# A decoder trunk on one core: sums of weight blocks in the MLPs moved from VectorE into accumulating DMAs

## The chip, the cores and the metric

The kernel runs on one core of one Trainium2 chip. The metric is the device time of one execution, in microseconds, and the median over the runs is given. The kernel is one program with fp32 inputs and outputs; TensorE (PE) works on fp32r operands, each value split into a high and a low part.

## The reference, cut to what matters

Two layers, the first with latent attention (MLA), the second with gated linear attention (GLA), each followed by an MLP on a residual stream of 512 tokens by 1024 channels:

```python
def sq_relu_mlp(xn, w_up, w_down):          # (512,1024), (1024,4096), (4096,1024)
    hid = jnp.square(jax.nn.relu(xn @ w_up))
    return hid @ w_down

for i in range(DEPTH):                       # DEPTH = 2
    ...
    x = x + mix.astype(x.dtype)
    x = x + sq_relu_mlp(rms_norm(x, norm_mlp[i]), mlp_w_up[i], mlp_w_down[i]).astype(x.dtype)
return rms_norm(x, final_norm)
```

Only the two MLPs are touched by the change.

## The kernel before, in words

**Split products.** An fp32 operand is split by `split`: ScalarE (ACT) copies it to a high part in fp32r (line 112), VectorE (DVE) subtracts that from the operand to get the low part (line 115). A product is then three matmuls: high by high, high by low, low by high. `piece` does this for a weight slice, into buffers `wh` and `wl` of which there are three each.

**Seven products in place of eight.** In each MLP both matrix products are done by a Winograd form of Strassen's scheme on 2 x 2 blocks: the tokens are cut into a first and a second half, the 1024 channels into two halves, and a weight block of `FB` = 512 hidden columns into two halves of 256. The weight blocks are called a11, a12, a21, a22. Seven products of blocks and of sums of blocks give the four results. The sums of the token side (T1 to T4, made by `combine` and `combined`) are formed once for each MLP, with the norm's gains in them; the sums of the weight side are formed for each block, on VectorE:

- step s5: s = a21 + a22 (line 904)
- step s6: s = s - a11 (line 919)
- step s3: a12 = a12 - s (line 925)
- step s7: a21 = a11 - a21 (line 932)

`up_block(b)` gives the steps of hidden block b (0 to 7): s1 (product with a11), s5, s2 (with a12), s6, s3, s7, s4 (with a22). A product of an up step is 24 matmuls of 256 columns (line 818). Steps s6, s7 and s4 add to one PSUM bank (`b2`), and VectorE reads it in between: after s7 (line 935) for one result, after s4 for the other. `finish` applies the norm's factor, the max with zero (line 862, VectorE) and the square (line 863, ScalarE).

`down_block(s)` does the same for the second product, with the hidden blocks 2s and 2s+1, in seven steps of 48 matmuls each: p1, p5, p6, p7, p2, p3, p4. Its weight quarters are 512 x 512 and are called "11", "21", "12", "22"; the sums over them are in p5 (line 987: S = 21 + 22), p6 (line 992), p7 (line 1004: 21 = 11 - 21) and p3 (line 1019). `operand` splits the hidden side into one of two buffers, h1 and h0 in turn. Only blocks 0 to 5 go this way; blocks 6 and 7 are multiplied plainly by `down` and `down_final`.

**Order.** In `mlp`, blocks 0 and 1 come first: s0 (their a11 and a12 are split early), then s1 of both, the last channel tile's token sums, the norm's mean and its factor, then s2 of both; then the rest of block 0, of block 1, and so on. From block 2 on a down step is put in behind every second up step, and one behind s4 of odd blocks. In blocks 0 and 1 there is none. The order of the instructions on each engine is fixed when the program is built; VectorE and ScalarE work through theirs in order, and the DMA queues of SyncE (SP) and GpSimd (POOL) too.

**Loads.** All weights come by SP's queue. Up slices (a11, a12, a21, a22, 512 KB each) go into five buffers `raw` of the pool `up`, one of which is also taken for s in each block. For blocks 0 and 1, a21 and a22 come together as one transfer of 1 MB each (line 1116) into two of the three `raw` buffers of the pool `down_w`; the third takes the first down quarter (line 950), and further quarters (1 MB each) take the three in turn. POOL's queue carries two small loads at the start of the program (`pos_i`, `invf`).

**Places.** `PADS` are unused bytes that shift the pools behind them. In the program before, h1 and h0 both start at 192 mod 512 bytes of their partition, the weight slices `wh` and `wl` at 416, the token operands of the up products (x, T) at 96, the `raw` buffers of `down_w` at 416.

Of the kernel before, what the change touches and what calls it, by code (L numbers as in the profile page):

```python
# [49 lines left out]
def trunk_kernel(ctx: ExitStack, tc: tile.TileContext, t_in: dict, out: bass.AP, out_row: bass.AP):  # L50
# [39 lines left out]

    PADS = dict(stage=224, right=64, up=320, masks=256, keep=128, hidden=(0, 0), down_w=(224, 224))

# [7 lines left out]
    opened_stage()  # L100
    pad(opened("edge", "right"), PADS["right"])
    opened("wide", "right")
# [163 lines left out]
    class QuadNorm(Norm):  # L266
# [36 lines left out]
        def difference(self, k):  # L303
            DVE.tensor_tensor(xT[k][:, second], xT[k][:, second], xT[k + KH][:, second], ALU.subtract)

# [480 lines left out]
    def out_proj(w2d, X, nxt, after, begun=None):  # L786
        for c in range(4):
            if c == 0:
                ps_, rest = begun or out_start(w2d, X, 0)
                rest()  # L790
            else:
                w = out_cols(w2d, c)
                if c == 3:
                    next(after)
                ps_ = [bank("ac"[c % 2]), bank("ac"[c % 2])]
                for j in range(2):
                    a_type(ps_[j], w[j], X)
            for j in range(2):
                m = c + j * KH
                DVE.tensor_tensor(xT[m], ps_[j], xT[m], ALU.add)  # L800
                nxt.add(m, xT[m])
            if c < 3:
                nxt.pair(c)
                nxt.difference(c)


    def mlp(layer, nrm, nxt, final=False):
# [5 lines left out]
        def wide_raw():  # L813
            return pool_of("down_w").tile([P, 4, 512], F32, tag="raw", bufs=3, name=uname("raw"))

        def matmuls(p, w, k0, ks, ms, x, begin, end):
# [18 lines left out]

        Q, wide, turn = {}, {}, [0, 1]

        def up_block(b):
# [7 lines left out]
            def unit(half, trail):  # L846
                if half and b < 2:
                    return wide[b][:, trail * KH : trail * KH + KH]
                t = up.tile([P, KH, 256], F32, tag="raw", bufs=5, name=uname("raw"))
                c0 = b * FB + half * 256  # L850
                with tc.issue_after(wide["last"].ins) if wide else nullcontext():
                    SP.dma_start(t, w_up[trail * 512 : trail * 512 + 512, c0 : c0 + 256].rearrange("(k p) n -> p k n", p=P))
                return t

            def product(p, a, name, begin):
# [3 lines left out]
            def finish(c, half, tk):  # L859
                qs = q[tk is second][:, 2 * half : 2 * half + 2]  # L860
                r = nrm.rstd[:, tk].unsqueeze(1).to_broadcast([P, 2, TH])
                DVE.scalar_tensor_tensor(qs, c, 0.0, r, ALU.max, ALU.mult)  # L862
                ACT.activation(qs, qs, AF.Square)  # L863
# [36 lines left out]
            def s5():  # L900
                s = v["s"] = up.tile([P, KH, 256], F32, tag="raw", bufs=5, name=uname("raw"))
                if "a12" not in v:
                    v["a12"] = unit(0, 1)
                DVE.tensor_tensor(s, v["a21"], v["a22"], ALU.add)  # L904
# [11 lines left out]
            def s6():  # L916
                if b == 1:
                    seed(v["p1"])
                DVE.tensor_tensor(v["s"], v["s"], v["a11"], ALU.subtract)
                product(v["b2"], v["s"], "T2", False)  # L920
# [3 lines left out]
            def s3():  # L924
                DVE.tensor_tensor(v["a12"], v["a12"], v["s"], ALU.subtract)  # L925
                product(v["x5"], v["a12"], "22", False)
# [4 lines left out]
            def s7():  # L931
                DVE.tensor_tensor(v["a21"], v["a11"], v["a21"], ALU.subtract)  # L932
                product(v["b2"], v["a21"], "T3", False)
# [10 lines left out]
        def down_block(s):  # L944
            last = s == NB // 2 - 2

            def quarter(dh, fh):
                t = wide_raw()
                r0 = (2 * s + fh) * FB
                SP.dma_start(t, w_dn[r0 : r0 + FB, dh * 512 : dh * 512 + 512].rearrange("(k p) n -> p k n", p=P))  # L950
                return t
# [9 lines left out]
            def product(n, a, t, evac=None):  # L961
# [11 lines left out]
                elif begin and n in (2, 3, 4, 5):  # L973
                    DVE.tensor_tensor(acc[n], p4, acc[n], ALU.add)
                else:
# [9 lines left out]
            def p5():  # L985
                v["21"], v["S"] = quarter(1, 0), quarter(1, 1)
                DVE.tensor_tensor(v["S"], v["21"], v["S"], ALU.add)
                DVE.tensor_tensor(b11, b12, b11, ALU.subtract)  # L988
                product(5, v["S"], b11)

            def p6():
                DVE.tensor_tensor(v["S"], v["S"], v["11"], ALU.subtract)
                DVE.tensor_tensor(b11, b22, b11, ALU.subtract)

# [8 lines left out]
            def p7():  # L1003
                DVE.tensor_tensor(v["21"], v["11"], v["21"], ALU.subtract)
                DVE.tensor_tensor(b12, b22, b12, ALU.subtract)
# [12 lines left out]
            def p3():  # L1018
                DVE.tensor_tensor(v["S"], v["12"], v["S"], ALU.subtract)
                product(3, v["S"], b22)  # L1020

            def p4():
                a = quarter(1, 1)
                DVE.tensor_tensor(b21, b21, b11, ALU.subtract)
                product(4, a, b21)
# [16 lines left out]
        def down(b, hid):  # L1042
            for c in range(2):
                raw = raw_rows(b, c)
                for g in range(2):
# [3 lines left out]
                    for j in range(2):  # L1049
                        m = c * 4 + g * 2 + j  # L1050
                        p = bank("b")
                        a_type(p, w, hid, cols=slice(j * P, (j + 1) * P))
                        DVE.tensor_tensor(xT[m], p, xT[m], ALU.add)
                        if b == NB - 1:
# [58 lines left out]
        for b in range(2):  # L1113
            t = wide[b] = wide_raw().rearrange("p a (b n) -> p (a b) n", b=2)
            c0 = b * FB + 256
            wide["last"] = SP.dma_start(t, w_up[:, c0 : c0 + 256].rearrange("(k p) n -> p k n", p=P))
        kept = tc.keep_in_program_order
# [8 lines left out]
        nrm.finish()  # L1126
        nrm.difference(KH - 1)
        for b in range(2):
# [421 lines left out]
    turns = rope_turns()  # L1550

    O, begun = mla(0, nrm, w0, mla_pools)
# [161 lines left out]
```

## Time and profile before

| | |
|---|---|
| median of 3 runs | 1080.58 us (1080.05 to 1083.18) |
| the profiled execution's own time | 1080.79 us |
| its span, first to last instruction | 1079.1 us |
| instructions of VectorE | 1210, busy 890.0 us |
| bytes read from HBM | 104.64 MB |
| stretch of the first MLP, of the second | about 190 to 470 us, about 743 to 1025 us |

The profile is one execution. A busy share of an engine is an average over stages of different kinds; the windows (busy time of each engine in a stretch) are the view by stage. An idle time stands with what ended it. Matmuls are pipelined: a row's duration of about 0.28 us is longer than the distance to the next one's start.

### The profile page before, as it was taken

What the parts mean: (1) busy time and instruction counts of PE and PEld (TensorE: products, weight loads), DVE (VectorE), ACT (ScalarE), POOL (GpSimd) and SP (SyncE); (2) the same over time, 40 slices, a digit from 0 to 9 for tenths busy, and PEclk for the clock granted to TensorE, in tenths of its full rate; (3) what the DMA queues carried; (4) which work ended last, traced back from release to release, by engine and by line L of the source; (5) the groups of instructions that cost most, each with busy time, mean ns of one, the idle gap of its engine ahead of it and who ended that gap; (6) DMA issues with size and microseconds to landing.
All of it is one profiled execution on the core that took longest, in us unless ns stands there. A gap on an engine that the chain in (4) does not pass through costs nothing.

```text
span 1079.1 us, 17824 instructions
## 1 busy us (share of the span) xinstructions
PE 1058.9 (98%) x7322; PEld 977.1 (91%) x7322; DVE 890.0 (82%) x1210; ACT 640.2 (59%) x934; POOL 44.5 (4%) x78
## 2 busy tenths in 40 slices
PE   9999999989999999999999999999899999999997
PEld 7788888989999999988788888888899999999986
DVE  6789879999899899967565655678999899899865
ACT  6577655566667776644334735655565667766734
POOL 6400000000000000030000000000000000000000
PEclk9999999999999999999999999999999999999999
DMA  7312017143433433260222222234324423522412
GB/s 211 95 49 79 13 31 229 42 136 99 157 98 99 157 100 96 86 203 24 62 67 78 79 79 57 61 98 138 117 79 129 146 82 134 176 76 82 137 39 79
DMA packets 97969, 107.88 MB, mean 100 GB/s; under 512 B 8048, under 2 KB 72832, under 8 KB 97888
## 3 DMA queue, kind: packets, MB, share of 16 engines
q1 hardware_dynamic: 95872, 105.52, 31.1%
q8 instruction: 57, 0.93, 0.4%
q10 hardware_dynamic: 1952, 1.21, 0.4%
q0 software_dynamic: 64, 0.02, 0.1%
q14 instruction: 24, 0.20, 0.1%
HBM read 104.64 MB, written 2.10 MB: 99 GB/s over the span
## 4 chain that ended last, share of the span: by engine, by line
PE 84%; DVE 11%; issue 2%; ACT 2%; DMA 1%; SPq 0%; DVEq 0%; ACTq 0%
PE ps L818 39%; PE ps L120 12%; PE ps L122 12%; PE ps L121 12%; DVE wl L115 4%; PE ps L137 2%; PE ps L1371 2%; DMA wraw_ckv<-in_mla_w_in_dram 1%; DVE q L862 1%; DVE h L115 1%; DVE raw L925 1%; ACT wh L112 1%; DVE raw L932 1%; DVE raw L904 0%; PE ps L1408 0%
## 5 line engine op out<-in xcount | busy, mean ns | idle before, releaser
L112 ACT ACTIVATE wh<-raw 128x1024 fp32r<-128x1024 f32 x208 | 218.9, 1057 | 155.2 <-PE ps L818 84.3
L115 DVE TENSOR_TENSOR wl<-raw,wh 128x1024 fp32r<-128x1024 f32 x208 | 251.8, 1218 | 16.6 <-ACT wh L112 16.3
L818 PE MATMUL ps<-h,wh 128*128 128x256 f32 x1344 | 170.6, 279 | 0.0
L818 PEld LDWEIGHTS ps<-h,wh 128*128 128x128 f32 x1344 | 163.0, 188 | 0.0
L818 PE MATMUL ps<-h,wl 128*128 128x256 f32 x672 | 92.3, 279 | 2.1 <-DVE wl L115 2.1
L120 PE MATMUL ps<-set,wh 128*128 128x512 f32 x232 | 92.0, 397 | 0.7 <-ACT set L245 0.7
L121 PE MATMUL ps<-set,wh 128*128 128x512 f32 x232 | 91.2, 393 | 0.6 <-DVE set L246 0.6
L122 PE MATMUL ps<-set,wl 128*128 128x512 f32 x232 | 91.1, 393 | 0.0
L112 ACT ACTIVATE wh<-wraw 128x1024 fp32r<-128x1024 f32 x41 | 43.0, 1056 | 74.0 <-PE ps L122 41.5
L818 PEld LDWEIGHTS ps<-h,wl 128*128 128x128 f32 x672 | 84.5, 188 | 2.5 <-DVE wl L115 2.5
L863 ACT ACTIVATE q<-q 128x512 f32<-128x512 f32 x64 | 40.0, 629 | 46.4 <-DVE q L862 46.2
L120 PE MATMUL ps<-wh,set 128*128 128x512 f32 x144 | 59.7, 414 | 0.0
L115 DVE TENSOR_TENSOR wl<-wraw,wh 128x1024 fp32r<-128x1024 f32 x41 | 50.3, 1230 | 10.7 <-ACT wh L112 10.6
L115 DVE TENSOR_TENSOR h<-q,h 128x1024 fp32r<-128x1024 f32 x44 | 53.6, 1220 | 4.9 <-ACT h L112 4.9
L122 PE MATMUL ps<-wh,set 128*128 128x512 f32 x144 | 56.3, 391 | 0.0
L121 PE MATMUL ps<-wl,set 128*128 128x512 f32 x144 | 56.3, 391 | 0.0
L121 PEld LDWEIGHTS ps<-set,wh 128*128 128x128 f32 x232 | 44.0, 190 | 10.5 <-DVE set L246 1.3
L120 PEld LDWEIGHTS ps<-set,wh 128*128 128x128 f32 x232 | 43.9, 190 | 10.0 <-ACT set L245 1.0
L122 PEld LDWEIGHTS ps<-set,wl 128*128 128x128 f32 x232 | 44.0, 190 | 9.0
L112 ACT ACTIVATE h<-q 128x1024 fp32r<-128x1024 f32 x44 | 46.2, 1052 | 4.8 <-DVE q L988 2.1
L818 PE MATMUL ps<-T0h,wh 128*128 128x256 f32 x128 | 33.2, 283 | 7.1 <-DVE q L935 6.7
L120 PE MATMUL ps<-hh,wh 128*128 128x512 f32 x96 | 37.4, 389 | 0.0
(512 smaller groups left out, 2778.2 us busy)
## 6 DMA issues: line engine op xcount, KB each, us to landing
raw<-in_mlp_w_down_dram SPq DMA_DIRECT2D x38, 1024.0 KB, 5.2
raw<-in_mlp_w_up_dram SPq DMA_DIRECT2D x56, 512.0 KB, 3.9
wraw<-in_gla_w_in_dram SPq DMA_DIRECT2D x11, 1024.0 KB, 5.1
wraw<-in_mla_w_o_dram SPq DMA_DIRECT2D x8, 512.0 KB, 4.8
raw<-in_mlp_w_up_dram SPq DMA_DIRECT2D x4, 1024.0 KB, 8.0
wraw<-in_gla_w_o_dram SPq DMA_DIRECT2D x8, 512.0 KB, 4.9
xT<-in_x_dram SPq DMA_DIRECT2D x6, 256.0 KB, 7.5
wraw_qn<-in_mla_w_uq_dram SPq DMA_DIRECT2D x6, 256.0 KB, 3.4
```

Source lines behind the costliest of these rows:

```text
L112: raised.append(order(ACT.activation(hi, src, AF.Copy)))
L115: return lo_eng.tensor_tensor(lo, src, f(hi), ALU.subtract)
L120: PE.matmul(psum, wh, xh, start=start, stop=False, **kw)
L121: PE.matmul(psum, wh, xl, start=False, stop=False, **kw)
L122: PE.matmul(psum, wl, xh, start=False, stop=stop, **kw)
L137: PE.transpose(psum, src, ident[: src.shape[0], : src.shape[0]])
L818: return PE.matmul(p[:, m * TH : (m + 1) * TH], w[i][:, k - k0, m * P : (m + 1) * P], x[k][j], start=start, stop=stop, skip_group_check=True,)
L862: DVE.scalar_tensor_tensor(qs, c, 0.0, r, ALU.max, ALU.mult)
L863: ACT.activation(qs, qs, AF.Square)
L925: DVE.tensor_tensor(v["a12"], v["a12"], v["s"], ALU.subtract)
L932: DVE.tensor_tensor(v["a21"], v["a11"], v["a21"], ALU.subtract)
L1371: PE.matmul(p[:, t * 64 : (t + 1) * 64].rearrange("p (n c) -> p n c", c=m), k[:, sl], later, start=True, stop=True)
```

## The change

The weight sums of s5 (blocks 0 and 1), of s7 (all blocks) and of p7 are no longer made by VectorE. Instead the second summand is read from HBM once more by a DMA on POOL's queue that adds it to what stands in the buffer (`accum_op=ALU.add`). The DMA adds, so a21 becomes a11 + a21 where it was a11 - a21, and signs are turned round elsewhere: on the token side (`combine` takes the negated gains `less`, `difference` becomes `total`), in `finish` (min with zero for half of the columns, since the square follows), in the sums of p4, p5, p6, p3, and where results are added to x. Two of these become a `scalar_tensor_tensor` with -1.0 in place of a `tensor_tensor`.

For blocks 2 to 7 the DMA goes out behind s5's sum, which reads a21. For blocks 0 and 1 all is loaded ahead, in `fill_sums`: s gets a21 by SP and then a22 added by POOL; a second buffer gets a21 and then a11 added; a third gets a22. These six halves fill all three `raw` buffers of `down_w`. The gains negated (`less`) are made once, early in the program, by one VectorE instruction of 16 columns. Pads: `right` goes, its 64 bytes being those of `less`; `hidden` becomes 416 bytes in the first MLP and 160 in the second, put between h1 and h0; `down_w` becomes 0 and 64.

```diff
-    PADS = dict(stage=224, right=64, up=320, masks=256, keep=128, hidden=(0, 0), down_w=(224, 224))
+    PADS = dict(stage=224, up=320, masks=256, keep=128, hidden=(416, 160), down_w=(0, 64))
...
+            l1, l2 = (less[:, self.g0 + j : self.g0 + j + 1] for j in (k, k + KH))
...
-            DVE.scalar_tensor_tensor(t2, u[:, first], g1, t3, ALU.mult, ALU.add)
-            DVE.scalar_tensor_tensor(t4, v[:, first], g2, t2, ALU.mult, ALU.subtract)
-            DVE.scalar_tensor_tensor(t1, v[:, second], g2, t2, ALU.mult, ALU.subtract)
+            DVE.scalar_tensor_tensor(t2, u[:, first], l1, t3, ALU.mult, ALU.subtract)
+            DVE.scalar_tensor_tensor(t4, v[:, first], l2, t2, ALU.mult, ALU.subtract)
+            DVE.scalar_tensor_tensor(t1, v[:, second], l2, t2, ALU.mult, ALU.subtract)
...
+            def fill(t, half, trail):
+                with tc.issue_after(wide["last"].ins) if "last" in wide and b > 1 else nullcontext():
+                    i = SP.dma_start(t, rows(half, trail))
+                if half and b < 2:
+                    wide["last"] = i
+                return t
+
+            def fill_sums(s):
+                v["s"] = s
+                fill(s, 1, 0)
+                joint(s, 1, 1)
+                fill(wide[b][0], 1, 0)
+                joint(wide[b][0], 0, 0)
+                fill(wide[b][1], 1, 1)
+
+            def joint(t, half, trail):
+                POOL.dma_start(t, rows(half, trail), accum_op=ALU.add)
...
             def s5():
-                s = v["s"] = up.tile([P, KH, 256], F32, tag="raw", bufs=5, name=uname("raw"))
-                if "a12" not in v:
+                if "s" not in v:
+                    v["s"] = up.tile([P, KH, 256], F32, tag="raw", bufs=5, name=uname("raw"))
                     v["a12"] = unit(0, 1)
-                DVE.tensor_tensor(s, v["a21"], v["a22"], ALU.add)
+                    DVE.tensor_tensor(v["s"], v["a21"], v["a22"], ALU.add)
+                    joint(v["a21"], 0, 0)
+                s = v["s"]
...
             def s7():
-                DVE.tensor_tensor(v["a21"], v["a11"], v["a21"], ALU.subtract)
                 product(v["b2"], v["a21"], "T3", False)
...
             def p5():
                 v["21"], v["S"] = quarter(1, 0), quarter(1, 1)
                 DVE.tensor_tensor(v["S"], v["21"], v["S"], ALU.add)
-                DVE.tensor_tensor(b11, b12, b11, ALU.subtract)
+                POOL.dma_start(v["21"], rows(0, 0), accum_op=ALU.add)
+                DVE.tensor_tensor(b11, b11, b12, ALU.subtract)
...
             def p7():
-                DVE.tensor_tensor(v["21"], v["11"], v["21"], ALU.subtract)
...
         for b in range(2):
-            t = wide[b] = wide_raw().rearrange("p a (b n) -> p (a b) n", b=2)
-            c0 = b * FB + 256
-            wide["last"] = SP.dma_start(t, w_up[:, c0 : c0 + 256].rearrange("(k p) n -> p k n", p=P))
+            wide[b] = halves(wide_raw())
+        for b, t in enumerate(halves(wide_raw())):
+            fills[b](t)
```

More of the change, by code (lines that the diff above doesn't have):

```diff
@@ L100, in trunk_kernel @@
     opened_stage()
-    pad(opened("edge", "right"), PADS["right"])
+    less = opened("edge", "right").tile([P, 16], F32, name="gains_less")
     opened("wide", "right")
@@ L834, in matmuls @@
                 one(1, 0, k, m, False, end and k == 3)
[L836 removed]
+        Q, wide, turn, fills = {}, {}, [0, 1], []
         def up_block(b):
@@ L918, in s6 @@
                     seed(v["p1"])
-                DVE.tensor_tensor(v["s"], v["s"], v["a11"], ALU.subtract)
+                DVE.tensor_tensor(v["s"], v["s"], v["a11"], ALU.add)
                 product(v["b2"], v["s"], "T2", False)
@@ L924, in s3 @@
             def s3():
-                DVE.tensor_tensor(v["a12"], v["a12"], v["s"], ALU.subtract)
+                DVE.tensor_tensor(v["a12"], v["a12"], v["s"], ALU.add)
                 product(v["x5"], v["a12"], "22", False)
@@ L973, in product @@
                 elif begin and n in (2, 3, 4, 5):
-                    DVE.tensor_tensor(acc[n], p4, acc[n], ALU.add)
+                    DVE.tensor_tensor(acc[n], p4, acc[n], ALU.add if n < 4 else ALU.subtract)
                 else:
@@ L1018, in p3 @@
             def p3():
-                DVE.tensor_tensor(v["S"], v["12"], v["S"], ALU.subtract)
+                DVE.tensor_tensor(v["S"], v["12"], v["S"], ALU.add)
                 product(3, v["S"], b22)
@@ L1052, in down @@
                         a_type(p, w, hid, cols=slice(j * P, (j + 1) * P))
-                        DVE.tensor_tensor(xT[m], p, xT[m], ALU.add)
+                        DVE.tensor_tensor(xT[m], p, xT[m], ALU.subtract if b < NB - 1 and m >= KH else ALU.add)
                         if b == NB - 1:
@@ L1550, in trunk_kernel @@
     turns = rope_turns()
+    DVE.tensor_scalar(less, gains[:, GAIN_COL["mlp"] : GAIN_COL["mlp"] + 16], -1.0, None, ALU.mult)
     O, begun = mla(0, nrm, w0, mla_pools)
```

35 lines of the change are left out of this document (21 added, 14 removed).

## The prediction

> **What bounds the kernel now.** I read the page's busy times and chain first, then a table of windows over the two MLPs, then TensorE's waits.
>
> ```profile
> PE 1058.9 (98%) x7322; PEld 977.1 (91%) x7322; DVE 890.0 (82%) x1210; ACT 640.2 (59%) x934; POOL 44.5 (4%) x78
> PE 84%; DVE 11%; issue 2%; ACT 2%; DMA 1%; SPq 0%; DVEq 0%; ACTq 0%
> ```
>
> TensorE (PE) is busy 98% of the span, so whatever the change takes from VectorE (DVE) counts only where PE stands still for it. The chain gives VectorE 11%. The windows show where (columns: length, then PE, weight loads, VectorE, ScalarE, POOL busy with counts, granted clock, DMA share, GB/s):
>
> ```profile
> 203.00:217.00 14.00, 11.77 (x99) 11.38 (x98) 14.00 (x16) 7.60 (x10) 0.00 (x0) 1.00 0.33 93
> 217.00:233.00 16.00, 14.45 (x122) 14.11 (x123) 15.93 (x17) 11.31 (x14) 0.00 (x0) 1.00 0.57 184
> 233.00:300.00 67.00, 67.00 (x585) 67.00 (x584) 62.47 (x57) 39.87 (x46) 0.00 (x0) 1.00 0.35 111
> 431.00:446.00 15.00, 13.93 (x121) 13.73 (x120) 15.00 (x15) 9.23 (x13) 0.00 (x0) 1.00 0.23 72
> 750.00:770.00 20.00, 17.54 (x145) 16.78 (x143) 19.95 (x22) 10.76 (x15) 0.00 (x0) 1.00 0.22 58
> 770.40:774.50 4.10, 4.10 (x22) 4.10 (x23) 3.85 (x4) 2.51 (x3) 0.00 (x0) 0.60 0.95 319
> 788.00:872.00 84.00, 84.00 (x732) 84.00 (x732) 78.22 (x72) 50.34 (x58) 0.00 (x0) 1.00 0.36 114
> 872.00:909.00 37.00, 36.74 (x315) 36.46 (x315) 36.90 (x33) 26.08 (x30) 0.00 (x0) 1.00 0.27 86
> 987.00:1001.00 14.00, 13.33 (x116) 13.13 (x114) 14.00 (x14) 8.23 (x11) 0.00 (x0) 1.00 0.23 76
> ```
>
> At the front of each MLP (203 to 233, 750 to 788) and at its end (431 to 446, 987 to 1001) VectorE is full and PE has holes; between them (233 to 300, 788 to 872) PE is full and VectorE has 5 to 6 us in hand. There a matmul of 256 columns starts every 67.00 / 585 = 114.5 ns, and nothing that VectorE saves shortens that. One row is odd: in 770.4 to 774.5 the granted clock is 0.60, right behind a hole of PE. TensorE's own waits, and the chain where it runs on VectorE:
>
> ```profile
> PE ps L818 <- DVE q L935: 6.7, 4, 2.0
> PE ps L818 <- DVE wl L115: 2.4, 3, 1.1
> PE ps L818 <- ACT wh L112: 1.4, 3, 0.5
> ```
> ```profile
> 200.03 1.13 DVE raw L932
> ...
> 232.66 198.91 PE ps L818 x1726
> ...
> 439.52 1.13 DVE raw L932
> ...
> 444.65 1.14 DVE wl L115
> ...
> 881.03 2.20 DVE raw L1004
> ```
>
> These ten waits (10.5 us) are what the MLPs can give back, beside the slow clock. L932, an instruction that the change drops, stands in the chain at the front and at the end; one such costs 1.13 us of chain.
>
> **The change part by part.** Removed from VectorE:
>
> ```profile
> L932 DVE TENSOR_TENSOR raw<-raw,raw 128x1024 f32<-128x1024 f32 x16 | 19.5, 1219 | 0.1
> L904 DVE TENSOR_TENSOR raw<-raw x4: 1217/1218/1222, 198.2 to 761.5; 128x1024 f32<-128x1024 f32 x4
> L1004 DVE TENSOR_TENSOR raw<-raw,raw 128x2048 f32<-128x2048 f32 x6 | 13.7, 2283 | 0.0
> ```
>
> 16 sums of step s7, 4 sums of s5 (blocks 0 and 1 of each MLP) and 6 of the down step p7: 19.5 + 4.9 + 13.7 = 38.1 us of VectorE, 19 per MLP. Most of it lies where PE is full, and is worth nothing. Wait by wait:
>
> ```profile
> 217.02 0.36 PE L818 MATMUL ps<-T0h,wh 128*128 128x256 f32 x1 [1.77 <-DVE q L935]
> L935 DVE TENSOR_TENSOR q<-ps,mt x16: 679/683/686, 216.2 to 1011.8; 128x512 f32<-128x512 f32 x16
> 445.84 0.62 PE L818 MATMUL ps<-h,wl 128*128 128x256 f32 x3 [1.07 <-DVE wl L115]
> ```
>
> (1) L935, four times, 6.7 us: s4 of blocks 0 and 1 may not add to its bank before VectorE has read it (L935), and in these blocks no down step lies between s7 and s4. Even with VectorE free, PE must wait for the 0.68 of L935 and some 0.2 of hand-over: 0.9 each, 3.6 stay and 3.1 go. In front of them four instructions go per MLP (two L904, two L932), 4 x 1.13 = 4.5 us of a VectorE that is late by 0.7 to 1.1, so I take it as in time.
> (2) L115, three times, 2.4 us: two are the ends at 445 and 1001 (1.07 each), behind the L932 of block 7; 1.13 less covers them. The third (before 909) has an L932 and L1004 ahead of it. An idle row understates a wait, since a matmul's row lasts 0.28 and the next could start 0.114 after it: 0.165 more each, so 2.4 + 0.5, less 0.3 left over: 2.6.
> (3) L112, three times: 1.4 + 0.5 = 1.9, ScalarE waiting behind L904 and L925, which come 1.1 to 4.5 us earlier. All goes.
> (4) The slow clock: 4.10 x 0.40 = 1.6 us lost, behind the longest hole (2.0). With holes of 0.9 I expect none; bounds 0 and 1.6.
> Together 9.2 us, at most 12.1 with the waits of (1) gone too, at least 4.5 if only (2) and (3) go.
>
> Added: 26 accumulating transfers on POOL's queue, 20 of 512 KB and 6 of 1 MB, and plain ones on SP's: for blocks 0 and 1 six of 512 KB in place of two of 1 MB. No row shows an accumulating transfer. The nearest:
>
> ```profile
> raw<-in_mlp_w_down_dram SPq DMA_DIRECT2D x38, 1024.0 KB, 5.2
> raw<-in_mlp_w_up_dram SPq DMA_DIRECT2D x56, 512.0 KB, 3.9
> raw<-in_mlp_w_up_dram SPq DMA_DIRECT2D x4, 1024.0 KB, 8.0
> pos_i<-in_positions_dram POOLq DMA_DIRECT2D x1, 2.0 KB, 4.5
> invf<-in_inv_freq_dram POOLq DMA_DIRECT2D x1, 16.0 KB, 6.9
> ```
>
> Ends for 512 KB: 3.9 (plain) and 3.9 + 6.9 = 10.8 (plain behind POOL's slowest issue). I take 3.9 + 4.5 = 8.4. The Trainium skill's "DMA: Bandwidth & Descriptors" (Anatomy of one DMA — SWDGE (gpsimd) path) fits 2.0 us plus bytes / 436 GB/s, an estimate of 3.2 us for a plain 512 KB; no run here shows one from this queue, and it would change nothing below.
>
> What hides them: from block 2 on the sum of s5 is read by s7 at least two up products (2.7 us each) and two down products (5.6 each) later, some 16 us, and for the down step likewise; 8.4 (or about 10 for 1 MB) fits. POOL's queue holds nothing else in the MLPs. In the first blocks the chain is longer:
>
> ```profile
> 177.35 1.00 SPq L1116 DMA_DIRECT2D raw<-in_mlp_w_up_dram  x2
> 214.56 0.37 SPq L950 DMA_DIRECT2D raw<-in_mlp_w_down_dram  x1
> ```
> ```profile
> 203.08 0.28 PE L818 MATMUL ps<-T0h,wh 128*128 128x256 f32 x1
> ```
>
> The first fill goes out at 177.35 and lands at the latest 8.0 later, 185.4. Then POOL's four accumulates follow: in series at 8.4 they land at 193.8, 202.2, 210.6 and 219.0. PE's 24-matmul products take 24 x 0.1145 = 2.75 us; the one that reads block 0's s starts at 203.08 and block 1's, five products on, at 216.8. Splitting takes 2.5 us ahead of a product, so the deadlines are 201 (s), 208 (its s7), 214 and 222: all met, with 3 us at the least. Both third-buffer halves are now taken by s, so the first down quarter waits for a buffer until 214.6, which is when the second was issued before; its product begins at 241. Cost taken: 0. The 18 MB of second reads fit a DMA share of 0.35. `less` is one small VectorE instruction early on, shorter than the 0.68 of a 512-wide one (I take 0.1). The sign changes keep each instruction's kind and count.
>
> The buffers' places: in the program before, both h buffers lie at 192 mod 512 and the weight slices at 416 (288 apart), the up operands at 96 (192 apart). The pads 416 and 160 move the second h buffer to 192 apart in MLP one and 448 in MLP two; the title's 288 is then the first buffer, unmoved. The first row is two h pieces, the second two up products, 48 matmuls each:
>
> ```profile
> 240.94:246.55 5.61, 5.61 (x51) 5.61 (x50) 5.61 (x6) 2.70 (x4) 0.00 (x0) 1.00 0.01 3
> 246.55:252.00 5.45, 5.45 (x50) 5.45 (x49) 5.45 (x5) 3.81 (x6) 0.00 (x0) 1.00 0.31 98
> ```
>
> 116.9 against 113.5 ns. In MLP one 10 of 21 operands, 480 matmuls, go to the faster distance: 480 x 3.4 = 1.6 us less. For 448 there is no row: between 1.6 less and 1.6 more, taken as 0. By the Trainium skill's "TensorE: Matmul & The Clock Gate" (Step-by-step: what each phase is for) loading the next weights takes no read bandwidth from the running matmul; by that the pads are worth 0 and the sum is 1.6 us slower. The two rows differ by 3.4 ns with PE full in both, so I go by the rows.
>
> Sum against the profiled execution's 1080.79 (span 1079.1, so 1.7 around it): 9.2 + 1.6 - 0.1 = 10.7 less, 1070.1. The median of the runs is 0.2 lower: 1069.9.
>
> **The rivals.**
> R1, only part of the stalls goes. VectorE's order is fixed when the kernel is built, and another order around L935 may keep those four waits and the slow clock: 4.5 + 1.6 goes, 1074.7. For it: L935 is bound to PE's own end. Against: VectorE loses 4.5 us of work before it.
> R2, more goes: the places are worth more (448 as good as 192) and all of (1) vanishes: 12.1 + 3.2, 1065.5.
> R3, nothing moves: what VectorE gives, another wait takes, or the second buffer in MLP two is as far off as the first gained; within 3 us of 1080.6.
> R4, slower: the accumulates come late. In series they are in time as long as each takes under some 9 us; past that the fourth is late by 4 t - 36.6 in each MLP. Both MLPs' lateness eats the 10.7 at t = 10.5, and at 12 us each it is 2 x 11.4 = 23 against 10.7: 1092. The same place has a harsher form: POOL cannot put out transfers while VectorE is busy, and in 203 to 217 it is busy 14.00 of 14.00. Then block 1's s, due at 214, comes at 233 or so, 19 late twice: 1108. "SBUF — State Buffer" of the Trainium skill (SBUF: two separate sides) has this trap for VectorE's 2-port modes, and says elsewhere that tensor_tensor has none. An L904 takes 1218 ns for 1024 elements, no doubled rate, which is against the harsh form; the long end of the bound, 10.8, is for the mild one.
>
> **How the numbers follow.** Forecast as reckoned (1066 to 1073.5): 0.53. R1 (1073.5 to 1077.3): 0.16. R2 (under 1066): 0.11. R3: 0.08. R4: 0.12. A measurement of this kernel can tell some 0.3%, 3.2 us, from no change, so faster 0.53 + 0.16 + 0.11 = 0.80, same 0.08, slower 0.12. The range leaves out R4, most of R3 and the far end of R2: 1063 to 1078.
>
> **What would show it.** L932 and L1004 as sums gone from VectorE's groups, its busy time near 852; POOL's queue with 16.8 MB more. Right: the front windows with PE full but for four holes near 0.9 us, the ends without the 1.07, no stretch of clock 0.60. The second h buffer's pieces in MLP one at 113.5 ns, and in MLP two a new number between 110 and 120. Wrong: PE or ScalarE waiting for a DMA of raw between 200 and 230, the accumulates' landings over 9 us; or the four L935 waits still near 1.7.

## The result, and the profile after

The changed kernel takes 1072.65 us (median; 1071.37 to 1073.91), against 1080.89 for the kernel before on the same chip: a ratio of 0.992 (95% interval 0.990 to 0.9941), 8.2 us faster. The forecast was 1069.9. The profiled execution has a span of 1070.3 us, 8.8 less than before.

The page of the changed kernel: busy times, the accumulating queue, and the four groups of transfers of the MLPs' weights (count, size, median us from issue to landing).

```profile
PE 1052.6 (98%) x7322; PEld 971.6 (91%) x7322; DVE 856.6 (80%) x1185; ACT 640.3 (60%) x934; POOL 77.7 (7%) x104
...
q0 software_dynamic: 13792, 16.80, 10.2%
...
raw<-in_mlp_w_down_dram SPq DMA_DIRECT2D x38, 1024.0 KB, 5.1
raw<-in_mlp_w_up_dram SPq DMA_DIRECT2D x68, 512.0 KB, 5.3
...
raw<-in_mlp_w_up_dram POOLq DMA_DIRECT2D x20, 512.0 KB, 6.5
raw<-in_mlp_w_down_dram POOLq DMA_DIRECT2D x6, 1024.0 KB, 9.2
```

VectorE lost 33.4 us of busy time, and TensorE only 6.3. (The lengths of VectorE's rows add up to 38.1 us less, as reckoned; neighbouring rows overlap at their ends, which busy time counts once and the expected 852 left out.) The transfers that now do the sums land in 6.5 and 9.2 us. TensorE's waits inside the MLPs (us in total, times, longest); L963 is the old L935, L937 the copy of the T1 product:

```profile
PE ps L825 <- DVE q L963: 4.8, 4, 1.5
...
PE ps L825 <- ACT mt L937: 0.9, 1, 0.9
...
PE ps L825 <- DVE wl L115: 0.7, 2, 0.3
```

The two large waits at the MLPs' ends are down to 0.3 each and ScalarE's L112 is gone from the list. But the four waits for L963 still take 4.8 of their 6.7 us, and one for L937 is new.

Where the 8.8 us went is read by setting TensorE's matmuls side by side: both programs issue the same 7322 in nearly the same order, so the start of the k-th in one less its start in the other is the gain up to there. The forecast's terms stand beside it:

| stretch | measured, us less | forecast |
|---|---|---|
| front of MLP one (198 to 237 us) | 0.6 | 2.2 |
| front of MLP two (744 to 797) | 3.3 | 4.4 |
| full stretches, MLP one / MLP two | 1.5 / 1.4 | 1.6 / 0 |
| ends of both MLPs, and 889 to 913 | 2.9 | 2.6 |
| before MLP one and behind MLP two | 0.8 more | 0.1 more |

(The fronts' 3.1 of L935 is halved here, of the 1.9 of L112 one wait in three is MLP one's, and the 1.6 of the slow clock is MLP two's: 6.6 in all, against 3.9.) A hole below is the distance between two matmuls' starts less one matmul's own, so it is some 0.165 us longer than the same wait in a list of waits. The last row is scatter for the most part: the first 73 us alone differ by up to 2 us between profiles of kernels that are identical there. Numbers for a stretch below leave it out.

The full stretches, where nothing waits, in windows of TensorE alone (length, busy time with matmuls started, clock, DMA share, GB/s). Before:

```profile
300.00:430.00 130.00, 130.00 (x1131) 1.00 0.36 114
810.00:890.00 80.00, 80.00 (x697) 1.00 0.38 120
```

After:

```profile
300.00:430.00 130.00, 130.00 (x1140) 1.00 0.55 146
810.00:890.00 80.00, 80.00 (x702) 1.00 0.53 146
```

The same 130 us hold nine matmuls more, 114.0 ns each and not 114.9, at the same full clock. That is the buffers' places; the second reads of the weights (DMA share 0.36 to 0.55) cost nothing there. From the starts of the 24 matmuls of each product: operands in the second hidden buffer went from 116.8 to 113.3 ns in MLP one (distance 192) and 113.8 in MLP two (448); the first buffer, unmoved at 288, stayed at 116.75. The 113.8 is a mean of two values: 18 of the 20 products take 113.3, and the last two, behind the hole at the MLP's end, 117.8.

### The profile page after: what moved, and what is told of

It reads as the page before. It is cut to its first block, busy times and chain, and to the rows that moved or that the text cites. A ratio compares the mean times of both kernels' runs of the same rounds, so it can differ in the third digit from the quotient of the medians.

```text
span 1070.3 us, 17930 instructions
## 1 busy us (share of the span) xinstructions
PE 1052.6 (98%) x7322; PEld 971.6 (91%) x7322; DVE 856.6 (80%) x1185; ACT 640.3 (60%) x934; POOL 77.7 (7%) x104
## 5 line engine op out<-in xcount | busy, mean ns | idle before, releaser
L112 ACT ACTIVATE wh<-raw 128x1024 fp32r<-128x1024 f32 x208 | 219.6, 1058 | 145.5 <-PE ps L825 98.0
L115 DVE TENSOR_TENSOR wl<-raw,wh 128x1024 fp32r<-128x1024 f32 x208 | 251.3, 1219 | 25.7 <-ACT wh L112 25.3
L112 ACT ACTIVATE wh<-wraw 128x1024 fp32r<-128x1024 f32 x41 | 43.0, 1056 | 78.0 <-PE ps L122 41.5
L878 POOL DMA_DIRECT2D raw<-in_mlp_w_up_dram x20 | 25.8, 1290 | 706.0 <-DVE raw L931 342.6
L115 DVE TENSOR_TENSOR h<-q,h 128x1024 fp32r<-128x1024 f32 x44 | 53.7, 1221 | 9.4 <-ACT h L112 9.4
L115 DVE TENSOR_TENSOR wl<-wraw,wh 128x1024 fp32r<-128x1024 f32 x41 | 50.4, 1231 | 10.6 <-ACT wh L112 10.5
L121 PEld LDWEIGHTS ps<-set,wh 128*128 128x128 f32 x232 | 43.6, 188 | 10.7 <-DVE set L246 1.7
L112 ACT ACTIVATE h<-q 128x1024 fp32r<-128x1024 f32 x44 | 46.1, 1049 | 0.6 <-DVE q L1020 0.6
```

Source lines behind the costliest of these rows:

```text
L112: raised.append(order(ACT.activation(hi, src, AF.Copy)))
L115: return lo_eng.tensor_tensor(lo, src, f(hi), ALU.subtract)
L121: PE.matmul(psum, wh, xl, start=False, stop=False, **kw)
L878: POOL.dma_start(t, rows(half, trail), accum_op=ALU.add)
```

## The experiments

All times are medians; ratios are to the kernel before in the same session, with their 95% intervals. The changed kernel's is 0.992 (0.990 to 0.9941). The sessions ran on different chips (the kernel before took 1080.9 to 1081.6 us in those with more than one execution), so small differences are read from the traces. The planner is the program that fixes each engine's order when the kernel is built.

**The places undone.**

```
-    PADS = dict(... hidden=(416, 160), down_w=(0, 64))
+    PADS = dict(... hidden=(0, 0), down_w=(224, 224))
```

> The changed kernel with the two places as before (hidden pads 0 and 0, down_w 224 and 224); all DMA accumulates stay. Theory A, the places are worth 1.6 us in MLP one and 1.4 us in MLP two, because the second hidden buffer's matmuls fell from 116.8 to 113.3 and 113.8 ns: about 1075.6 us, 3.0 above the changed kernel, growing evenly along the full stretches, with that buffer back at 116.8 ns. Rival B, the places are worth nothing and the 3 us are a side effect of the accumulates (fewer VectorE reads): 1072.6, and the second buffer stays near 113.5 ns. The prediction's own taking (1.6 and 0): 1074.2.

1074.04 us, ratio 0.9931 (0.9919 to 0.9943). Its full stretches:

```profile
300.00:430.00 130.00, 130.00 (x1131) 1.00 0.54 145
810.00:890.00 80.00, 80.00 (x698) 1.00 0.53 146
```

The count is back at 1131 with the DMA share still 0.54, and both buffers are at 116.75 ns. The running difference grows by 1.7 us in MLP one and 1.6 in MLP two: theory A, 3.2 us in all. The time alone, 1074.04, would have spoken for the prediction's own taking (1074.2). It shows about half, because the new wait at L937 is gone in this kernel (1.2 us): nothing but the addresses was changed, yet the order that the planner gives VectorE at the front came out otherwise.

**The first two blocks' sums back on VectorE.**

```
-                    joint(v["a21"], 0, 0)
+                    if b > 1:
+                        joint(v["a21"], 0, 0)
...
             def s7():
+                if b < 2:
+                    DVE.tensor_tensor(v["a21"], v["a11"], v["a21"], ALU.add)
...
-            wide[b] = halves(wide_raw())
-        for b, t in enumerate(halves(wide_raw())):
-            fills[b](t)
+            t = wide_raw()
+            wide[b] = halves(t)
...
+            wide["last"] = SP.dma_start(joined(t), w_up[...])
```

> The changed kernel, but the sums of the first two blocks of each MLP are made on VectorE again, from two 1 MB loads as before; the later accumulates and the places stay. Theory A, read from the distance between the two kernels' matmuls: the fronts brought 0.4 us in MLP one and 3.1 in MLP two (the slow clock at 770 to 774 us among them): about 1076.1 us. Rival B, the prediction's split: both fronts brought 6.6 us together (3.1 + 1.9 + 1.6), so about 1079. Rival C, MLP one's front brought more than 0.4 and lost it to the late rsqrt: 1077, with 1.08 us of wait at 209 us gone and larger waits before it.

1075.02 us, ratio 0.9935 (0.9922 to 0.9948); the span is 3.3 longer, 0.8 of it in MLP one's front and 2.4 in MLP two's. Theory A, a little short; the prediction's 6.6 for the fronts is too much. Its waits, and a window with the clock (the last three columns are clock, DMA share, GB/s):

```profile
PE ps L825 <- DVE q L967: 5.9, 4, 1.8
...
PE ps L825 <- DVE wl L115: 1.4, 2, 1.1
PE ps L825 <- ACT wh L112: 0.9, 2, 0.5
```
```profile
214.00:218.00 4.00, 2.15 (x18) 1.95 (x17) 4.00 (x6) 1.69 (x2) 0.00 (x0) 1.00 0.65 224
218.00:222.00 4.00, 4.00 (x23) 4.00 (x22) 2.44 (x4) 1.84 (x3) 0.00 (x0) 0.57 0.56 176
```

ScalarE's L112 waits are back, and so is a stretch at a low clock (0.57 over the 4 us), this time in MLP one, again behind a hole of 2.0 us. MLP one's 0.8 is a difference: the wait at L937 is gone (1.2 gained by 211 us), as rival C expected, and 2.0 is lost between 211 and 237 us, most of it to the low clock. Taking four sums per MLP off the front was worth only 1.1 us of the four L963 waits (5.9 against 4.8).

**The sums of blocks 2 to 5 and of the first two down blocks back on VectorE**, then the up sums alone.

```
-                    joint(v["a21"], 0, 0)
+                    if b > 5:
+                        joint(v["a21"], 0, 0)
...
             def s7():
+                if 1 < b < 6:
+                    DVE.tensor_tensor(v["a21"], v["a11"], v["a21"], ALU.add)
...
-                POOL.dma_start(v["21"], rows(0, 0), accum_op=ALU.add)
+                if last:
+                    POOL.dma_start(v["21"], rows(0, 0), accum_op=ALU.add)
...
             def p7():
+                if not last:
+                    DVE.tensor_tensor(v["21"], v["11"], v["21"], ALU.add)
```

> The changed kernel, but the sums of blocks 2 to 5 and those of the first two down blocks are made on VectorE again (8 up sums of 1.13 us and 4 down sums of 2.2 us over both MLPs, some 18 us of VectorE's time). Theory A, PE is full there and VectorE has slack: 1072.6 us, no change beyond 0.5. Rival B, every sum that VectorE sheds counts somewhere because its queue is what PE waits for: up to 18 us, 1090. Rival C, the accumulates cost something in the full stretch (longer landing times of the loads behind them): faster than the changed kernel, about 1071.

1077.11 us, ratio 0.9959 (0.9944 to 0.9973), span 5.1 longer: not nothing, and far from 18. The last stretch before the end of MLP two (PE, weight loads, VectorE, ScalarE, POOL), this kernel first, then the changed one:

```profile
870.00:910.00 40.00, 38.90 (x336) 38.53 (x335) 39.90 (x36) 27.99 (x34) 0.00 (x0) 1.00 0.27 81
```
```profile
870.00:910.00 40.00, 40.00 (x352) 40.00 (x352) 38.27 (x35) 28.46 (x33) 1.28 (x1) 1.00 0.56 156
```

Here VectorE had slack only until about 870 us: with the sums it is busy 39.90 of 40, as in the kernel before, and TensorE stands 1.1 us; by the running difference the stretch costs 1.9 (idle time understates a hole, and the three products between its holes run at 117.8 ns and not at 113.3). The rest is 0.3 us at 354, 1.7 in both fronts (2.3 at the last wait for the old L935, 0.6 of it got back, for the most part because MLP two's front leaves 117.8 ns at 768 us and not at 781), and 1.2 ahead of MLP one's first product, where VectorE's order came out otherwise.

> The changed kernel with the up sums of blocks 2 to 5 on VectorE again (8 of 1.13 us over both MLPs); the four down sums stay with the DMA. With both kinds back the span was 5.1 us longer: 1.2 before MLP one's first sum, 2.3 at the T3 sums of block 1, 2.0 between 354 and 906 us. Theory A, VectorE's queue is full between 870 and 910 us when it does both (39.90 of 40 us), and the down sums of 2.3 us are what fills it: the 2.0 us go, about 1075. Rival B, the planner's order moves with any sum put back, whatever the load: some other set of 0.5 to 1.2 us waits, 1072 to 1077, with VectorE not full where they lie. Rival C, the up sums count as they did: 1077.5 with the same waits.

1076.1 us, ratio 0.9939 (0.9926 to 0.9952); the profiled execution is the slowest of the six (1072.87 to 1077.63). The losses at 354 and in 870 to 910 are gone (theory A for those; VectorE is busy 39.86 of 40 there and TensorE full), those at the fronts' last wait stayed (theory C for those). VectorE at that place, start and length of each row, with block 2's sum on it:

```profile
229.91 1.23 DVE L963 TENSOR_TENSOR raw<-raw,raw 128x1024 f32<-128x1024 f32 x1
231.04 0.69 DVE L958 TENSOR_TENSOR q<-ps,mt 128x512 f32<-128x512 f32 x1
231.64 1.22 DVE L115 TENSOR_TENSOR wl<-raw,wh 128x1024 fp32r<-128x1024 f32 x1
232.78 0.69 DVE L889 SCALAR_TENSOR_TENSOR q<-q,rstd 128x512 f32<-128x512 f32 x1
233.38 1.23 DVE L115 TENSOR_TENSOR h<-q,h 128x1024 fp32r<-128x1024 f32 x1
234.51 0.69 DVE L966 TENSOR_TENSOR q<-ps,mt 128x512 f32<-128x512 f32 x1
```

and in the changed kernel:

```profile
228.21 1.22 DVE L115 TENSOR_TENSOR h<-q,h 128x1024 fp32r<-128x1024 f32 x1
229.35 0.68 DVE L957 TENSOR_TENSOR q<-ps,mt 128x512 f32<-128x512 f32 x1
229.95 1.22 DVE L115 TENSOR_TENSOR wl<-raw,wh 128x1024 fp32r<-128x1024 f32 x1
231.08 0.69 DVE L889 SCALAR_TENSOR_TENSOR q<-q,rstd 128x512 f32<-128x512 f32 x1
231.69 0.68 DVE L963 TENSOR_TENSOR q<-ps,mt 128x512 f32<-128x512 f32 x1
```

The lines moved by three: block 2's sum is L963 in the first fence and the awaited instruction L966. The sum takes the slot of the hidden operand's split (L115 h), and that split, 1.13 us, falls between TensorE's last T3 matmul and the instruction that it waits for (L966): a wait of 2.2 instead of 1.15 us. The same hole of 2.2 in MLP two is followed by a stretch at a low clock (0.57 over 4 us) in this kernel and by none in the one before it.

**The norm's factor ahead of block 0's second sum.**

```
-        DVE.scalar_tensor_tensor(r, b, 1.5, y0, ALU.add, ALU.mult)
+        rs_last[0] = DVE.scalar_tensor_tensor(r, b, 1.5, y0, ALU.add, ALU.mult)
...
-                DVE.tensor_tensor(v["s"], v["s"], v["a11"], ALU.add)
+                with tc.issue_after(rs_last[0].ins) if b == 0 else nullcontext():
+                    DVE.tensor_tensor(v["s"], v["s"], v["a11"], ALU.add)
```

> The changed kernel with one edge more: VectorE's second sum of block 0 in each MLP (the line that adds a11 to s) is queued behind the last step of the norm's factor. In MLP two the order is that already. Theory A, the new 1.08 us wait at 209 us in MLP one (TensorE for the fifth product's operand, which waits for the squares of the first outputs) comes from two sums put ahead of the factor: it goes, and the time is about 1071.5. Rival B, the sums that are now later make the third and fourth products wait instead: 1072.6 or above, with a VectorE wait between 203 and 208 us.

VectorE in the changed kernel, MLP one's front:

```profile
201.31 1.22 DVE L948 TENSOR_TENSOR raw<-raw,raw 128x1024 f32<-128x1024 f32 x1
202.44 0.68 DVE L218 SCALAR_TENSOR_TENSOR mt<-ps,mt 128x512 f32<-128x512 f32 x1
203.04 1.22 DVE L954 TENSOR_TENSOR raw<-raw,raw 128x1024 f32<-128x1024 f32 x1
204.18 0.68 DVE L220 SCALAR_TENSOR_TENSOR mt<-mt,mt 128x512 f32<-128x512 f32 x1
204.78 1.22 DVE L115 TENSOR_TENSOR wl<-raw,wh 128x1024 fp32r<-128x1024 f32 x1
205.91 0.68 DVE L221 SCALAR_TENSOR_TENSOR rstd<-mt,mt 128x512 f32<-128x512 f32 x1
...
207.65 1.28 DVE L889 SCALAR_TENSOR_TENSOR q<-ps,rstd 128x512 f32<-128x512 f32 x2
...
215.68 1.22 DVE L948 TENSOR_TENSOR raw<-raw,raw 128x1024 f32<-128x1024 f32 x1
216.81 0.68 DVE L963 TENSOR_TENSOR q<-ps,mt 128x512 f32<-128x512 f32 x1
```

The planner puts two sums (L948, L954) and a split (L115) ahead of and between the steps of the factor (L218, L220, L221), and rstd comes some 3 us late: at 206.6, against 203.5 in the kernel before. That s comes early from the DMA allows this but is not shown to cause it: with the places undone s comes in the same way, and there neither sum stands between the steps; the kernel before had two sums there too (L904, L932). ScalarE squares the outputs of L889 before the copy L937, and TensorE waits for the copy. With the edge, rstd is done at 203.9 and TensorE's hole at 209 us falls from 1.08 to 0.36: 0.7 us less in that front, 1072.19 us, ratio 0.991 (0.9897 to 0.9923). The time alone would not tell it from the changed kernel; the trace does. Theory A. The last two rows show block 0's L963 wait: block 1's sum L948 stands ahead of it, so that wait is 1.5 and not 0.9.

**TensorE's order in the first two blocks.**

```
             def s6():
                 if b == 1:
-                    seed(v["p1"])
+                    made[0]["s4"]()
                 DVE.tensor_tensor(v["s"], v["s"], v["a11"], ALU.add)
+                if b == 1:
+                    ... (block 1's third product, then seed)
...
+                    if b == 2:
+                        made[1]["s4"]()
```

> The changed kernel with TensorE's order altered in the first two blocks of each MLP: block 0's last product (T4) follows block 1's T1 product, block 1's third product precedes its T2 product, and block 1's T4 product follows block 2's first. So another product of 2.7 us runs while VectorE adds up the T3 product's bank. Theory A, the four waits of 4.8 us for that sum are the rest of the gain that the change left, and nothing but TensorE's order keeps them: they go, and the time falls by 4 to 5 us to about 1068 us. Rival B, VectorE is full there (20.7 of 23 us between 210 and 233 us), so that the next operand is late instead: same time as the changed kernel, 1072.6, with waits for the operands' rounding (wl, wh) in their place.

1069.89 us, ratio 0.9888 (0.9876 to 0.9901), span 2.1 less. All four L963 waits are gone, without a wait for operands in their place, but two others came (L957; L939 is the copy that was L937):

```profile
PE ps L825 <- ACT mt L957: 1.5, 2, 0.7
...
PE ps L825 <- ACT mt L939: 0.9, 1, 0.9
```

Block 1's T3 product now follows T2 directly and must wait until ScalarE has copied T2's bank (L957, 0.9 of hole each time): a place I had overlooked in the edit. In the two fronts it is 3.8 us less; 0.5 is given back at the end of MLP one, where this execution's matmuls take 117.8 ns, the rest outside the MLPs. Theory A by mechanism; the 4 to 5 us were too much.

**Both hidden buffers at the better distance.**

```
-                if turn[1:] == [1] and not turn[0]:
+                if turn[1:] == [1]:
                     turn.append(pad(dp, PADS["hidden"][layer]))
```

> The changed kernel with the place before the first hidden buffer, not between the two, so that both hidden buffers start at 96 (MLP one) or 352 (MLP two) modulo 512 and stand 192 or 448 from the weights. Theory A, the distance of the moving operand from the weights sets the 116.75 or 113.3 to 113.8 ns of a matmul: the first buffer's 21 products of 24 matmuls per MLP fall by 3.4 and 3.0 ns, 1.7 + 1.5 = 3.2 us less, 1069.4. Rival B, it takes two buffers at different places for the gain (one is written while the other is read): no gain or the second buffer back at 116.75 ns, 1072.6 to 1076.

1069.42 us, ratio 0.9886 (0.9873 to 0.9898), and 1149 matmuls in the window that held 1140; both buffers 113.34 ns:

```profile
300.00:430.00 130.00, 130.00 (x1149) 1.00 0.54 146
810.00:890.00 80.00, 80.00 (x708) 1.00 0.54 146
```

The full stretches are 1.6 and 1.8 us shorter: theory A. Distance decides, not the difference between the two buffers.

**The last three edits together** (the factor's edge, TensorE's order, both buffers).

> The altered product order of the first two blocks, the norm's factor ahead of block 0's second sum on VectorE, and both hidden buffers at the better place, on top of the changed kernel. Theory A, the parts add: 4.5 + 0.7 + 3.2 = 8.4 us less, about 1064.2. Rival B, with TensorE's waits gone VectorE becomes the bound at the ends of the fronts and takes some 2 to 3 us back: 1067.

1072.51 us, ratio 0.9928 (0.9906 to 0.995): neither theory. The nine executions fall into two groups, two at 1080.4 and 1080.7, seven from 1070.4 to 1073.1. The profiled one took 1080.67, and has fewer waits than any other kernel here (some 3.5 us of holes in both MLPs together, against some 9 in the changed one):

```profile
300.00:430.00 130.00, 130.00 (x1106) 1.00 0.53 142
810.00:890.00 80.00, 80.00 (x682) 1.00 0.54 147
```

At full clock every matmul of both stretches takes 117.75 ns. Looking back with that, the same 117.8 stands in stretches of every trace, the kernel before included, where an operand is 192 or 448 from the weights: from a wait up to a later wait or a product at another distance. In the changed kernel it is the front of MLP two from 747 to 780 us; a hole of 1.7 us at 766 leaves it, one of 0.95 at 781 ends it. So these distances have two values, 113.3 and 117.8, a hole may change the one into the other, and otherwise it persists. A product at 288 (116.7, but for two of some 480 that took 117.7 behind a hole) nearly always leaves 113.3 behind it: in all traces together 219 of the 229 products that followed one directly ran at 113.3, and nine of the other ten follow the hole at an MLP's end. Against the kernel with only the buffers moved, the running difference grows by 7.7 us in MLP one's stretch and 6.7 in MLP two's. 1080.5 less either is about 1073, so in the lower group one MLP may have run at 117.75; no execution of that group was profiled, and this stays open.

**One buffer back at 288, the two orders kept.**

```
-                if turn[1:] == [1]:
+                if turn[1:] == [1] and not turn[0]:
```

> The kernel with the altered product order and the norm's factor first, with the hidden buffers where the changed kernel has them: the first at 288 from the weights, the second at 192 or 448. Against the kernel with all three edits it differs in the first buffer's place alone. That one ran every matmul of both full stretches at 117.75 ns. Theory A: at 192 and 448 a matmul takes 113.3 or 117.8 ns, whichever it falls into behind a wait, and keeps that; a product whose operand stands at 288 (116.7 ns always) puts the next one at 113.3. So with the first buffer at 288 the stretches run at 116.7 and 113.3 again in every execution: 1070.3 - 2.1 (the order, as it ran alone) - 0.7 (the factor) is a span of 1067.5 us, some 1069 as a time, and no execution above 1072. Rival B: the 117.75 ns come with the two orders, wherever the buffer is: 1072 to 1080 as with all three edits, with the matmuls of the second buffer at 117.8.

1068.55 us (1067.43 to 1068.94), ratio 0.988 (0.9863 to 0.9896), span 1066.5:

```profile
300.00:430.00 130.00, 130.00 (x1140) 1.00 0.54 142
810.00:890.00 80.00, 80.00 (x703) 1.00 0.52 145
```

Theory A for the full stretches: 116.7 and 113.3 again, and none of the four executions above 1069. It is not a strict rule: behind the hole at MLP one's end (445 to 459 us) five products run at 117.8 although one at 288 comes right before them. This is the fastest version measured, 4 us ahead of the changed kernel; with both buffers at 192 and the old order (1069.42) it overlaps, but that one has no product at 288 to end a stretch at 117.8.

**Seven other distances**, in two kernels, one execution each. The edit puts a pad of its own size ahead of each hidden buffer.

> The changed kernel with other places for the hidden buffers, to read the time of a matmul at four distances (operand less weights, modulo 512) that no run has shown: in MLP one 384 and 64, in MLP two 320 and 128. Known so far: 288 gives 116.7 ns, 0 gives 120.0, 192 and 448 give 113.3 or 117.8, whichever they fall into. Theory A, it depends on the distance either way round (d like 512 - d): 320 as 192 and 64 as 448, so 113.3 or 117.8 for both, and between 113.3 and 120 for 384 and 128, alike. Theory B, nothing but 288 and 0 differs from the rest: all four 113.3 or 117.8, with long stretches of one value, since no product at 288 is left to end a slow stretch.

> As the other one, with 480 and 256 in MLP one, and 224 and 288 in MLP two (288 as in the changed kernel, 224 beside it). Theory A (d like 512 - d): 224 as 288, 116.7 ns in both buffers of MLP two; 480 near 0's 120 or 448's 113.3; 256 unknown. Theory B: 116.7 at 288 only, the others 113.3 or 117.8.

1080.31 and 1078.65 us (the kernel before 1083.46 beside them). The windows of the first kernel, then of the second:

```profile
300.00:430.00 130.00, 130.00 (x1122) 1.00 0.53 142
810.00:890.00 80.00, 80.00 (x692) 1.00 0.53 145
```
```profile
300.00:430.00 130.00, 130.00 (x1119) 1.00 0.53 142
810.00:890.00 80.00, 80.00 (x693) 1.00 0.54 146
```

The table below is from the starts of each product's matmuls. Theory A falls (224 takes 118.1, 288 takes 116.75) and so does B (128 and 384 take 118.9). All seven are slower than 288. The 0 is block 1's first product, in every kernel, whose weights stand in a token operand's place. That it is the distance which counts, and not the operand's own address, rests on that product: its operand starts at 96 mod 512 and takes 120.0 against weights at 96, and 113.3 or 117.8 against weights at 416. In all others the weights stay at 416.

| operand less weights, mod 512 bytes | ns per matmul |
|---|---|
| 192 (all kernels), 448 (MLP two) | 113.3 or 117.8 |
| 288 | 116.75 |
| 64, 320 | 117.8 |
| 224, 480 | 118.1 |
| 384, 128 | 118.9 (128 once 119.8, right behind a stretch at 117.8) |
| 256 | 119.6 |
| 0 | 120.0 |

## Why the prediction was right and where it was wrong

The direction and three quarters of the size were right: 8.2 us against 10.7. Part of the closeness is luck: the fronts gave 2.7 us less than reckoned, and 1.4 of that came back from MLP two's places, which were taken at 0. The steps:

- **(1) L935, "3.6 stay and 3.1 go": wrong.** 4.8 stay. The floor of 0.9 per wait held, or nearly, for block 1, but for block 0 VectorE's order has block 1's sum ahead of it (215.68 and 216.81 above), 1.5 each. The step assumed that a VectorE with fewer instructions would be in time; what counts is which instruction stands next in its fixed order when TensorE's last T3 matmul ends. The runs with the product order changed show that the waits themselves could be avoided.
- **(3) L112, "All goes": right for L112, but a wait took its place.** I did not ask what order the planner would give the new front: it put two sums and a split among the factor's steps, and L937 costs 1.2 us of hole in MLP one. With the edge, 0.7 of it goes. These two steps explain 2.4 of the 2.7 us missing at the fronts; MLP two's front at 117.8 ns (five products of 24 matmuls between 766 and 780 us, 4.4 ns each, 0.5) covers the rest.
- **(4) The slow clock: right in the outcome.** The changed kernel has clock 1.00 in 745 to 785, though the holes that were to shrink to 0.9 are still 1.7 at the longest. It came back in two experiments, each time behind a hole of 2.0 us or more.
- **(2) The ends: right**, 2.9 against 2.6, with 0.5 left at each end. The bound of 12.1 us and R2 with it add up the waits as the list has them; with the 0.5 added under (2) and under (3), and the 0.3 left over, it would be 12.8. No chance hangs on that.
- **"Most of it lies where PE is full, and is worth nothing": wrong as a rule.** Put back, the middle sums cost 5.1 of span: in 870 to 910 us, where VectorE has no slack, and at the seam where block 2's sum enters the front's order. In the sum of the forecast this did little harm, since the waits at both places stood under (1) and (2), but the sums that those waits hung on were the wrong ones.
- **The places.** MLP one right (1.5 to 1.7 against 1.6). MLP two was taken at 0 and is 1.4 to 1.6: 448 is as good as 192, the far end of the bound. The rival that the places are worth 0 doesn't fit the counts: 1131, 1140 and 1149 with nothing else moved. The Trainium skill's "TensorE: Matmul & The Clock Gate" (Step-by-step: what each phase is for) says that loading the next weights takes no read bandwidth from the running matmul; the rival was drawn from that, and why the address counts all the same no run here shows.
- **The accumulates: right that they are in time, wrong in how.** They land in 6.5 and 9.2 us, not 8.4 and 10. In MLP one they went out not after 177 but at 154.59 to 160.30, because their plain loads now leave SP's queue from 150.05 us on; these rows of POOL show it (start, length of the issue):

```profile
154.59 2.75 POOL L878 DMA_DIRECT2D raw<-in_mlp_w_up_dram  x2 [72.20 <-DMA raw<-in_mlp_w_up_dram]
158.80 1.28 POOL L878 DMA_DIRECT2D raw<-in_mlp_w_up_dram  x1 [1.45 <-DMA raw<-in_mlp_w_up_dram]
160.30 1.28 POOL L878 DMA_DIRECT2D raw<-in_mlp_w_up_dram  x1 [0.23 <-DMA raw<-in_mlp_w_up_dram]
```

R4 did not come about in either form. R1 described the fronts better than the forecast, except that the slow clock went. The sign changes were taken to keep every instruction's kind; 12 of VectorE's became the other kind, at the same 14.6 us. Undone one by one, the fronts' sums, the middle sums and the places lengthen the span by 3.3, 5.1 and 1.6 us (the first and the last with L937's 1.2 us got back); what each does alone can't be cut out cleaner than to about 1 us, because each edit draws another order for VectorE.

## What to carry to other kernels

Work taken off an engine whose order is fixed in advance is worth what stands next in that order at the end of each wait, so look up the instruction ahead of the awaited one before and after, and expect the planner to reorder at any edit, even one that moves nothing but addresses. Price the address of a matmul's operand against that of its weights: it was worth 3.4 ns in 117 and up to 6.7, and where a place has two values, keep products between whose place mostly ends the slow one. A wait that two rows of one bank force is removed by giving TensorE another product to run between them, not by speeding up the engine that it waits for.

## What the hardware showed that I had not expected

At distances 192 and 448 the same matmul runs at 113.3 or 117.8 ns with the clock granted in full, and keeps its value for up to 240 us; it changed only behind a hole of TensorE or a product at another distance. What sets it was not found.

In the MLPs, holes of 2.0 us or more were followed by a low clock in three of six cases, shorter ones never. Each time it is 0.50 for 3.41 us; the 0.57 and 0.60 above are means over windows of some 4 us. Within one profile the clock's changes lie whole multiples of 3.413 us apart. Cut into cells of that length, the traces tell the six holes apart by TensorE's idle time within one cell: 1.97, 1.85 and 2.05 us came before the low clock, and no cell in an MLP with 1.8 or less did. The two holes of 2.2 us without it, in the kernel with both kinds of middle sums back, are each split by a cell's end. A cell of the kernel before and the next one, then the fuller cell of such a split hole (TensorE busy, clock, DMA share, GB/s):

```profile
767.77:771.18 3.41, 1.44 (x13) 1.00 0.56 163
771.18:774.59 3.41, 3.41 (x19) 0.50 0.91 294
```
```profile
230.61:234.02 3.41, 1.92 (x17) 1.00 0.81 306
```

The third hole without it, in MLP one of the kernel with the up sums back, had 1.8 us of idle time in its cell. So 1.8 to 1.85 parts these cases, but it is no general limit: in the first 20 us of five profiles the low clock followed cells with 1.6 to 2.1 us of idle time. No edit moved a hole against the cells on purpose, so this is read from the traces and not tested.

POOL's accumulating transfer of 512 KB lands in 6.5 us although VectorE is nearly full, and the doubled reads of those weights left the matmuls' rate unchanged (1131 matmuls in 130 us at a DMA share of 0.36 and of 0.54).
